# Dots of fetched rows queued later, and a tail of three combinations in a one-layer diffusion backbone with expert retrieval

## The chip, the cores and the metric

The kernel runs on one core of a Trainium2 chip. Its engines are TensorE (PE, with its weight loads as PEld), VectorE (DVE), ScalarE (ACT), GpSimd (POOL) and SyncE (SP, which here issues DMAs only). The metric is the device time of one execution in microseconds.

## The reference

One layer over 512 latent tokens of width 1024 with a prefix of 256 context tokens: a token mixer (two groups of linear-attention heads), then retrieval over 128 x 128 experts with one neuron each. The change touches the second half:

```python
def peer(h, w_query, sub_keys, expert_u, expert_v):
    def block(t):                                    # 128 tokens
        q = (t @ w_query).reshape(PEER_BLOCK, PEER_HEADS, 2, PEER_DQ // 2)
        s1 = jnp.einsum('thd,nd->thn', q[:, :, 0], k1)
        s2 = jnp.einsum('thd,nd->thn', q[:, :, 1], k2)
        v1, i1 = lax.top_k(s1, PEER_TOPK)
        v2, i2 = lax.top_k(s2, PEER_TOPK)
        ...
        top_s, pos = lax.top_k(cand_s, PEER_TOPK)    # 16 of 256 pairs
        idx = jnp.take_along_axis(cand_i, pos, axis=-1)
        g = jax.nn.softmax(top_s, axis=-1)
        act = jax.nn.gelu(jnp.einsum('thkd,td->thk', expert_u[idx], t))
        return jnp.einsum('thk,thkd->td', g * act, expert_v[idx])
```

Each token thus weighs 8 x 16 = 128 experts. A modulated residual and a layer norm follow.

## The kernel before

The 512 tokens are four blocks of 128. For blocks 0 to 2 (384 tokens, `TD`) the retrieval is done densely: every expert's hidden value for every token by matmul, times a gate that is zero for experts that weren't chosen. For block 3, and for the u side of the last 16 tokens of block 2 (`SH`, the shared tokens), the chosen rows of u and v are fetched one at a time.

**The choice.** DVE finds the top 16 of each list (`top16`, `pick_head`) and then the keys of the chosen pairs (`picks`: one-hot `oh`, times `spread`, summed to `key`), for block 2, then 3, then 0; block 1 follows within the gate matrix. In this part the order on DVE is written out by hand (a manual schedule), for DVE and later for DVE and POOL.

**The hidden blocks.** `hidden(n)` (64 of them, n = 0 to 63, two groups of 128 experts each) loads a megabyte `ur`, splits it into a high part `uh` (ACT) and a low part `ul` (DVE) in `load_split`, and runs 48 matmuls of 128 x 368 into `pH`, three for each product (`mm3`, lines 139 to 141: the high parts, and each low part with the other high one). ACT applies the gelu; 28 of the results (`SPILL`) go to DRAM (`Hd`) and come back later.

**The gate matrix.** `gate_block` makes for each of the three blocks 16 groups of 8 tokens; a group takes a one-hot product on DVE (lines 1093, 1098, 1104), four scaled copies on ACT (line 1100), and 24 matmuls into `pG` (line 1110). The results go through `stage` to DRAM (`Gd`), and come back for eight expert groups at a time as `Gn` (1536 KB).

**The fetched rows.** `fetched` is a generator of 272 steps, each of one 4 KB row for each of 128 tokens (512 KB): 16 for the shared tokens (`sdots`), then 16 of u and 16 of v in turn, 8 times. POOL issues the fetches into a ring of six buffers (`erow`), the first five at once and another as each dot is issued. A dot on DVE (lines 1221, 1227) reduces a row of u; line 1239 adds a weighted row of v into `yg`. After the 16 shared dots ACT takes their gelu and spreads them with eight small DMAs from its own queue (line 1225). How many rows are asked for at each place is set by `ROWS`: per group of the gate matrix, per half of a combination while hidden blocks remain, and per half of one after that. Ahead of the gate matrix there are rows in the choice: four between the steps of `picks(w, 3)` and one at each of the six steps of `picks(w, 0)`.

**The main loop.** Combination i (m = seq[i]) loads and splits a megabyte of v (`rows`: `vr`, `vh`, `vl`), multiplies the stored hidden values by the gates and splits them (`gated`: `gel`, `ah`, `al`), and adds 36 matmuls of 128 x 512 into the six accumulators `y` (`combine`). The first stage (i = 0 to 31) runs hidden block 32 + i on PE ahead of combination i; after the last one the ring of u (`uring`) is closed, and a second ring for v (`vring`) takes its place. From then on the loads of v alternate between the pools w and vring, two raw buffers and one pair of split tiles each. In this second stage eight loads of `w_g2` (1/8 of the last modulation each) also go through vring.

**The tail.** The last `TAIL` combinations are prepared together, and then run by block, so that block 0's sums end first; `finish` (residual, modulation, layer norm, lines 1251 to 1253 and 134 to 135, all on DVE) follows for block 3 (the fetched one), then 0, 1 and 2. Its modulation rows need `to_rows` (a transpose on PE, a copy on ACT at line 270) and two small DMAs on POOL. In the tail the order on ACT is that of the program. Elsewhere a scheduler sets the order by priorities of the program order.

Of the kernel before, what the change touches and what calls it, by code (L numbers as in the profile page):

```python
# [931 lines left out]
class Peer:  # L932
# [14 lines left out]
    LOOK = 5  # L947
    ROWS = (1.0, 2.75, 0.75)
    GB, OB = 8, 2
    GN = 8  # L950
    TAIL = 2

# [172 lines left out]

    def load_split(self, pool, src, tag, bufs):

        nc = self.nc
        raw = pool.tile([128, 2, 8, 128], F32, name=tag + "r", bufs=2)
        nc.sync.dma_start(raw, src)  # L1130
        parts = []
        for e in range(2):
            hi, lo = (pool.tile([128, 8, 128], F32R, name=tag + i, bufs=bufs) for i in "hl")
            nc.scalar.activation(hi, raw[:, e], AF.Copy)  # L1134
            self.mark = nc.vector.tensor_tensor(lo, raw[:, e], hi, op=OP.subtract).ins  # L1135
            parts.append((hi, lo))
        return parts
# [24 lines left out]

    def gated(self, n, pool, vpool, bufs, mark=None):

        nc = self.nc
        NG, NU = self.TD // self.GT, self.TU // self.GT
        if 2 * n % self.GN == 0:
            self.Gn = pool.tile([128, NG, self.GN, self.GT], F32, name="Gn", bufs=2)
            nc.sync.dma_start(self.Gn, self.Gd[:, :, 2 * n:2 * n + self.GN, :].rearrange("g m n t -> m g n t"))
        g = self.gel.pop(n)  # L1170
        g4 = g.rearrange("p n (g t) -> p n g t", t=self.GT)
        m = 2 * n % self.GN
        gates = self.Gn[:, :, m:m + 2, :].rearrange("p g n t -> p n g t")
        nc.scalar.activation(g4[:, :, NU:], gates[:, :, NU:], AF.Copy)
        with self.tc.issue_after(mark) if mark else ExitStack():
            nc.vector.tensor_tensor(g4[:, :, :NU], g4[:, :, :NU], gates[:, :, :NU], op=OP.mult)
        ah = vpool.tile([128, 2, self.TD], F32R, name="ah", bufs=bufs)
        al = vpool.tile([128, 2, self.TD], F32R, name="al", bufs=bufs)
        nc.scalar.activation(ah, g, AF.Copy)  # L1179
        nc.vector.tensor_tensor(al, g, ah, op=OP.subtract)  # L1180
        return ah, al

    def rows(self, n, pool):

        return self.load_split(pool, self.a["vd"][n], "v", 2)

# [8 lines left out]
    def fetched(self, w, ring, y):  # L1195
# [21 lines left out]
        for r, (src, j) in enumerate(order):  # L1217
# [8 lines left out]
            elif src == "u":  # L1226
                nc.vector.scalar_tensor_tensor(e, e, 1.0, h2, op0=OP.mult, op1=OP.mult, accum_out=dots[:, j:j + 1])  # L1227
                if j == 15:

                    g = self.g[96:128, 2].rearrange("p h k -> p (h k)")  # L1230
                    nc.vector.tensor_tensor(g, g, act[96:128], op=OP.mult)
                if j % 16 == 15:
                    sl = slice(j - 15, j + 1)
                    nc.scalar.activation(act[:, sl], dots[:, sl], AF.Gelu_apprx_tanh)
                    nc.vector.tensor_tensor(act[:, sl], act[:, sl], self.g[:, 3].rearrange("p h k -> p (h k)")[:, sl], op=OP.mult)
# [23 lines left out]
    def run(self, es, out):  # L1259
# [6 lines left out]
        kept, out_to = self.AHEAD, self.AHEAD + self.SPILL  # L1266
        seq = [*range(kept), *range(out_to, 64), *range(kept, out_to)]
        self.gel, self.last = {}, 2 * seq[-1]
        pers = es.enter_context(tc.tile_pool(name="pers", bufs=1, reuse_waits="tile"))
# [4 lines left out]
        with ExitStack() as e0:  # L1274
# [5 lines left out]
            with ExitStack() as e1:  # L1280
# [58 lines left out]
                for i, _ in enumerate(self.picks(w, 3)):  # L1339
                    if i % 2:  # L1340
                        more(0.5)
                    if i > 1:
                        next(fetched)
                index()
# [12 lines left out]
                with tc.tile_pool(name="bd", bufs=1, reuse_waits="tile") as bp:  # L1357
                    for i, _ in enumerate(self.picks(w, 0)):
                        if i % 2:
                            more(0.5)  # L1360
                        fetch(1)
                    more(0.5)
                    first, at, groups = asked, 0, ND * 128 // self.GB
                    for b in range(ND):
                        kg = self.picks_on_partitions(bp, ps, key2 if b == 2 else self.key, self.g[:, b])
                        following = self.picks(w, 1) if b == 0 else iter(())
# [8 lines left out]
            with ExitStack() as e1:  # L1375
# [5 lines left out]
                g2 = iter(())  # L1381
                vp, pools = None, [w]
                for i, m in enumerate(seq[:64 - self.TAIL]):
# [3 lines left out]
                    if nh < 64:  # L1387
                        self.hidden(nh, up, gl, hps)
                        nh += 1
                        if nh == 64:  # L1390
                            up_es.close()
                            deep = e0.enter_context(ExitStack())
                            vp = deep.enter_context(tc.tile_pool(name="vring", bufs=1, side="right", reuse_waits="tile"))
                            pools.append(vp)
                            g2 = n.mods_last(vp)
                    else:
                        next(g2, None)
                    fetch(rate)
                    v = self.rows(m, pools[i % len(pools)])
                    if nh == 64 and i + ahead < 64:  # L1400
                        self.back(seq[i + ahead], gl)
                    ops = self.gated(m, w, w, self.TAIL, mark), v
                    for e in range(2):
# [9 lines left out]
                for c, m in enumerate(tail):  # L1413
                    mark = self.mark
                    vs.append(self.rows(m, pools[(64 - self.TAIL + c) % 2]))
                    acts.append(self.gated(m, w, w, self.TAIL, mark))

# [48 lines left out]
```

## Time and profile before

| | |
|---|---|
| median of 3 runs | 1776.82 us (1775.97 to 1776.92) |
| the profiled execution | 1778.75 us |
| its span | 1776.8 us, 27590 instructions |
| mean granted TensorE clock | 0.973 |
| moved by DMA | 439.13 MB, mean 247 GB/s |
| PE idle, 600 to 700 us of the span | 19.3 us |
| longest single PE wait | 15.8 us, for `ul` |

The busy time of an engine counts its instructions from start to end; matmuls overlap, so a PE that is busy all the time is not at its peak. What limits a stage is read from the wait that ends last there. In a row of the timeline the columns are start, duration, engine, line, operation, output and inputs, shapes, count, and in brackets the idle time of the engine just before and what ended it. "SPq" and "ACTq" are DMAs issued by these engines.

### The profile page before, as it was taken

Reading aid. Unit: us, or ns where it says so; the run is one execution under the profiler, and the core shown is the slowest. Engines: PE = TensorE matmul, PEld = TensorE weight load, DVE = VectorE, ACT = ScalarE, POOL = GpSimd, SP = SyncE. Lnnn points to the kernel's source line nnn. Section 1 sums busy time; section 2 is a strip of 40 time slices with the busy share of each in tenths; the row PEclk is TensorE's granted clock in tenths of the full one; section 3 lists DMA queues with packets and bytes.
Section 4 is the critical chain, followed back from the end, with each engine's and each line's share of the span. In section 5 each row is a group of like instructions: output and inputs, shape, how many; then the busy total and the mean of one; then the engine's idle time right before and its main releaser. Section 6 shows DMA issues by size and latency. Waiting matters only on the chain. (4 is left out here: it accounts for less than half of the span.)

```text
span 1776.8 us, 27590 instructions
## 1 busy us (share of the span) xinstructions
PE 1669.0 (94%) x10440; PEld 1460.4 (82%) x10440; DVE 1450.7 (82%) x2824; ACT 831.2 (47%) x1413; POOL 483.1 (27%) x327
## 2 busy tenths in 40 slices
PE   6999999989999978999998999999999998999994
PEld 3888877876788978889898889999999997778883
DVE  6689888787799979999897788787787776677756
ACT  4667677664322354667574333243333333233331
POOL 0000000000043023126432555545455452223000
PEclk8999999989999998899999999999999999999997
DMA  8345345143331367799889999989989989999832
GB/s 320 121 140 175 123 136 179 48 191 117 125 108 52 116 208 276 275 321 328 309 328 372 337 374 359 320 325 347 352 304 340 345 296 331 329 309 339 292 126 95
DMA packets 155687, 439.13 MB, mean 247 GB/s; under 512 B 13105, under 2 KB 69777, under 8 KB 135074
## 3 DMA queue, kind: packets, MB, share of 16 engines
q1 hardware_dynamic: 114322, 289.94, 47.0%
q0 software_dynamic: 40400, 145.34, 22.5%
q10 hardware_dynamic: 832, 2.11, 0.3%
q8 instruction: 81, 1.33, 0.3%
q14 instruction: 52, 0.43, 0.1%
HBM read 388.93 MB, written 48.39 MB: 246 GB/s over the span
## 5 line engine op out<-in xcount | busy, mean ns | idle before, releaser
L141 PE MATMUL pH<-hh,ul 128*128 128x368 f32 x1024 | 342.7, 336 | 22.2 <-DVE ul L1135 22.1
L139 PE MATMUL pH<-hh,uh 128*128 128x368 f32 x1024 | 344.1, 336 | 5.7 <-ACT gel L1153 4.7
L140 PE MATMUL pH<-hl,uh 128*128 128x368 f32 x1024 | 341.3, 333 | 0.0
L139 PE MATMUL y<-vh,ah 128*128 128x512 f32 x768 | 300.2, 391 | 9.3 <-ACT vh L1134 5.7
L141 PE MATMUL y<-vh,al 128*128 128x512 f32 x768 | 298.9, 390 | 2.0 <-DVE al L1180 2.0
L140 PE MATMUL y<-vl,ah 128*128 128x512 f32 x768 | 299.9, 391 | 0.9 <-DVE vl L1135 0.8
L1212 POOL DMA_INDIRECT erow<-in_v_dram,ix x128 | 218.4, 1706 | 239.0 <-DVE yg L1239 133.6
L1212 POOL DMA_INDIRECT erow<-in_u_dram,ix x128 | 197.3, 1541 | 311.3 <-DVE erow L1227 178.6
L1135 DVE TENSOR_TENSOR vl<-vr,vh 128x1024 fp32r<-128x1024 f32 x128 | 156.0, 1222 | 108.9 <-ACT vh L1134 108.7
L1134 ACT ACTIVATE uh<-ur 128x1024 fp32r<-128x1024 f32 x128 | 135.3, 1059 | 206.8 <-PE pH L140 179.0
L1134 ACT ACTIVATE vh<-vr 128x1024 fp32r<-128x1024 f32 x128 | 134.3, 1054 | 186.2 <-PE y L141 115.5
L141 PEld LDWEIGHTS pH<-hh,ul 128*128 128x128 f32 x1024 | 195.4, 191 | 24.7 <-DVE ul L1135 24.6
L139 PEld LDWEIGHTS pH<-hh,uh 128*128 128x128 f32 x1024 | 195.6, 191 | 7.8 <-ACT gel L1153 5.3
L140 PEld LDWEIGHTS pH<-hl,uh 128*128 128x128 f32 x1024 | 195.7, 191 | 1.2
L139 PEld LDWEIGHTS y<-vh,ah 128*128 128x128 f32 x768 | 144.4, 188 | 39.9 <-ACT vh L1134 6.0
L141 PEld LDWEIGHTS y<-vh,al 128*128 128x128 f32 x768 | 144.6, 188 | 33.2 <-DVE al L1180 2.9
L140 PEld LDWEIGHTS y<-vl,ah 128*128 128x128 f32 x768 | 144.5, 188 | 30.6 <-DVE vl L1135 2.0
L1239 DVE SCALAR_TENSOR_TENSOR yg<-erow,q,yg 128x1024 f32<-128x1024 f32 x127 | 162.4, 1278 | 0.3
L1135 DVE TENSOR_TENSOR ul<-ur,uh 128x1024 fp32r<-128x1024 f32 x128 | 154.4, 1217 | 9.9 <-ACT uh L1134 9.9
L1227 DVE SCALAR_TENSOR_TENSOR erow<-erow,h 128x1024 f32<-128x1024 f32 x128 | 151.9, 1217 | 0.1
L1180 DVE TENSOR_TENSOR al<-gel,ah 128x768 fp32r<-128x768 f32 x64 | 61.0, 954 | 72.3 <-ACT ah L1179 72.1
L139 PE MATMUL pc<-hTh,wh 128*128 128x512 f32 (+1 forms) x304 | 110.2, 362 | 0.3 <-ACT G L379 0.3
(397 smaller groups left out, 3062.6 us busy)
## 6 DMA issues: line engine op xcount, KB each, us to landing
ur<-in_uT_dram SPq DMA_DIRECT2D x64, 1024.0 KB
vr<-in_vd_dram SPq DMA_DIRECT2D x64, 1024.0 KB
Gd<-stage SPq DMA_DIRECT2D x24, 1024.0 KB
Gn<-Gd SPq DMA_DIRECT2D x16, 1536.0 KB
wraw<-in_w_cf_dram SPq DMA_DIRECT2D x24, 512.0 KB
wada<-in_w_ada_dram SPq DMA_DIRECT2D x48, 256.0 KB
Hd<-gels SPq DMA_DIRECT2D x28, 368.0 KB
gel<-Hd SPq DMA_DIRECT2D x28, 368.0 KB
```

Source lines behind the costliest of these rows:

```text
L139: mm(out, lh, rh, start=start, stop=False)
L140: mm(out, lh, rl, start=False, stop=False)
L141: mm(out, ll, rh, start=False, stop=stop)
L1134: nc.scalar.activation(hi, raw[:, e], AF.Copy)
L1135: self.mark = nc.vector.tensor_tensor(lo, raw[:, e], hi, op=OP.subtract).ins
L1180: nc.vector.tensor_tensor(al, g, ah, op=OP.subtract)
L1212: nc.gpsimd.indirect_dma_start(out=e, out_offset=None, in_=a["v" if src == "v" else "u"], in_offset=bass.IndirectOffsetOnAxis(ap=ix[:, j:j ...
L1227: nc.vector.scalar_tensor_tensor(e, e, 1.0, h2, op0=OP.mult, op1=OP.mult, accum_out=dots[:, j:j + 1])
L1239: nc.vector.scalar_tensor_tensor(y, e, act[:, j:j + 1], y, op0=OP.mult, op1=OP.add)
```

## The change

Four things:

- The four rows in `picks(w, 3)` and the six in `picks(w, 0)` are no longer asked for there. The first call of the generator, which issues five fetches, stays where it was. `ROWS` becomes 0.85, 2.85 and 0.83.
- The product of the shared tokens' gates and hidden values (`g` for the last 16 tokens of block 2) is taken after the fifth row of u instead of the sixteenth, since rows come later; an assertion makes sure that it comes before block 2's part of the gate matrix.
- `TAIL` is 3 instead of 2. The third combination of the tail keeps its split v (`home[:2]`) and its split gated values (`home[2]`) in the memory of `hh` and `hl`, the split input that only the hidden blocks read. The buffers for `ah` and `al` stay at two.
- The loads of v alternate counted from i = 31 (`first`), so that combination 31 uses pool w and combination 32 is the first in vring.

```diff
-    ROWS = (1.0, 2.75, 0.75)
+    ROWS = (0.85, 2.85, 0.83)
-    TAIL = 2
+    TAIL = 3
...
-    def load_split(self, pool, src, tag, bufs):
+    def load_split(self, pool, src, tag, bufs, home=None):
...
-            hi, lo = (pool.tile([128, 8, 128], F32R, name=tag + i, bufs=bufs) for i in "hl")
+            hi, lo = home[e] if home else (pool.tile([128, 8, 128], F32R, name=tag + i, bufs=bufs) for i in "hl")
...
-        ah = vpool.tile([128, 2, self.TD], F32R, name="ah", bufs=bufs)
-        al = vpool.tile([128, 2, self.TD], F32R, name="al", bufs=bufs)
+        if home:
+            ah, al = (t.rearrange("p a b -> p (a b)")[:, 0:2 * self.TD].rearrange("p (e t) -> p e t", e=2) for t in home)
+        else:
+            ah, al = (vpool.tile([128, 2, self.TD], F32R, name=f"a{i}", bufs=bufs) for i in "hl")
...
-                if j == 15:
+                if j == 4:
                     g = self.g[96:128, 2].rearrange("p h k -> p (h k)")
                     nc.vector.tensor_tensor(g, g, act[96:128], op=OP.mult)
+                    self.shared = True
...
                 for i, _ in enumerate(self.picks(w, 3)):
                     if i % 2:
                         more(0.5)
-                    if i > 1:
-                        next(fetched)
...
                     for i, _ in enumerate(self.picks(w, 0)):
                         if i % 2:
                             more(0.5)
-                        fetch(1)
...
                     for b in range(ND):
+                        assert b < 2 or self.shared
...
                             pools.append(vp)
+                            first = i
...
-                    v = self.rows(m, pools[i % len(pools)])
+                    v = self.rows(m, pools[(i - first) % len(pools)])
...
-                    ops = self.gated(m, w, w, self.TAIL, mark), v
+                    ops = self.gated(m, w, w, self.TAIL - 1, mark), v
...
-                    vs.append(self.rows(m, pools[(64 - self.TAIL + c) % 2]))
-                    acts.append(self.gated(m, w, w, self.TAIL, mark))
+                    home = c == self.TAIL - 1 and [
+                        [t[:, 2 * j:2 * j + 2, :].rearrange("p a (b c) -> p (a b) c", c=128) for t in (self.hh, self.hl)]
+                        for j in range(3)]
+                    vs.append(self.rows(m, pools[(64 - self.TAIL + c - first) % 2], home and home[:2]))
+                    acts.append(self.gated(m, w, w, self.TAIL - 1, mark, home and home[2]))
```

The order of DVE's instructions in the middle of the choice (`erow,sdots` is a dot of a shared row, `oh` and `key` are the one-hot products and the result for block 3, `pr`, `pf` and `prf` small steps for the next blocks). Before, the stretch that holds the first three dots; the pair of splits (`ul`) follows eight rows later:

```order
L1030 TENSOR_SCALAR pr<-pos_5224 128x128 x3
L1221 SCALAR_TENSOR_TENSOR erow,sdots<-erow,yg 128x1024
L1054 TENSOR_TENSOR oh<-oh,spread 128x2048
L1056 TENSOR_TENSOR oh<-oh 128x8x128
L1056 TENSOR_TENSOR oh<-oh 128x8x64
L1056 TENSOR_TENSOR oh<-oh 128x8x32
L1057 TENSOR_TENSOR key<-oh 128x128
L1221 SCALAR_TENSOR_TENSOR erow,sdots<-erow,yg 128x1024
L1052 TENSOR_TENSOR oh<-prf,iota_5231 128x2048
L1221 SCALAR_TENSOR_TENSOR erow,sdots<-erow,yg 128x1024
L1054 TENSOR_TENSOR oh<-oh,spread 128x2048
L1043 SCALAR_TENSOR_TENSOR prf<-pf 128x128
```

And after, the stretch that ends with the same pair of splits:

```order
L1052 TENSOR_TENSOR oh<-prf,iota_5231 128x2048
L1030 TENSOR_SCALAR pr<-pos_5224 128x128
L1054 TENSOR_TENSOR oh<-oh,spread 128x2048
L1043 SCALAR_TENSOR_TENSOR prf<-pf 128x128
L1056 TENSOR_TENSOR oh<-oh 128x8x128
L1045 TENSOR_TENSOR prf<-pf 128x128
L1056 TENSOR_TENSOR oh<-oh 128x8x64
L1030 TENSOR_SCALAR pr<-pos_5224 128x128
L1056 TENSOR_TENSOR oh<-oh 128x8x32
L1040 CAST pf<-pr 128x512
L1057 TENSOR_TENSOR key<-oh 128x128
L1135 TENSOR_TENSOR ul<-ur,uh 128x1024 x2
```

Three dots stood ahead of this pair of splits and none does now. Ten of the dots ahead of the gate matrix have moved into it or behind it: the first dot stands at the end of the choice for block 0.

The loads on SP where the first stage ends (`silr` and `wg` belong to the last modulation). Before, the first load of vring stands ahead of `silr`:

```order
L1130 DMA vr<-in_vd_dram 128x2048
L1161 DMA gel<-Hd 128x2x368
L1130 DMA vr<-in_vd_dram 128x2048
L255 DMA silr<-sild 128x1024
L259 DMA wg_15062<-in_w_g_dram 128x1024
L1130 DMA vr<-in_vd_dram 128x2048
```

And after:

```order
L1130 DMA vr<-in_vd_dram 128x2048
L1161 DMA gel<-Hd 128x2x368 x2
L255 DMA silr<-sild 128x1024
L259 DMA wg_15032<-in_w_g_dram 128x1024
L1130 DMA vr<-in_vd_dram 128x2048
```

The first load of vring now stands behind the first load of w_g2 instead of ahead of both.

ACT in the tail, up to the copy of the last modulation row (line 270). Before:

```order
L1134 ACTIVATE vh<-vr 128x1024 x2
L1174 ACTIVATE gel<-Gn 128x2x16
L1179 ACTIVATE ah<-gel 128x768
L270 ACTIVATE q_4773<-prow 8x128
L1424 ACT_TABLE_LOAD
```

And after:

```order
L1134 ACTIVATE vh<-vr 128x1024 x2
L1174 ACTIVATE gel<-Gn 128x2x16
L1181 ACTIVATE ah<-gel 128x768
L1134 ACTIVATE hh<-vr 128x1024 x2
L1174 ACTIVATE gel<-Gn 128x2x16
L1181 ACTIVATE hh<-gel 128x768
L270 ACTIVATE q_4773<-prow 8x128
```

The third combination's four instructions, written into hh, stand ahead of that copy.

More of the change, by code (lines that the diff above doesn't have):

```diff
@@ L1161, in back, with gated @@
             self.nc.sync.dma_start(r[:, :, :self.TU], self.Hd[n - self.AHEAD])
-    def gated(self, n, pool, vpool, bufs, mark=None):
+    def gated(self, n, pool, vpool, bufs, mark=None, home=None):
         nc = self.nc
@@ L1181, in gated, with rows @@
         return ah, al
-    def rows(self, n, pool):
-        return self.load_split(pool, self.a["vd"][n], "v", 2)
+    def rows(self, n, pool, home=None):
+        return self.load_split(pool, self.a["vd"][n], "v", 2, home)
     def combine(self, n, e, b, ops, halves=(0, 1)):
@@ L1267, in run @@
         seq = [*range(kept), *range(out_to, 64), *range(kept, out_to)]
+        self.shared = False
         self.gel, self.last = {}, 2 * seq[-1]
@@ L1381, in run @@
                 g2 = iter(())
-                vp, pools = None, [w]
+                vp, pools, first = None, [w], 0
                 for i, m in enumerate(seq[:64 - self.TAIL]):
```

## The prediction

> **What bounds the kernel now.** I read the page first, then the busy time by windows, then PE's own timeline, because the page says that PE is the engine to follow.
>
> ```profile
> PE 1669.0 (94%) x10440; PEld 1460.4 (82%) x10440; DVE 1450.7 (82%) x2824; ACT 831.2 (47%) x1413; POOL 483.1 (27%) x327
> 600.00:700.00 100.00, 80.74 (x462) 79.21 (x462) 86.05 (x248) 45.44 (x51) 27.97 (x27) 0.91 0.64 219
> 1200.00:1300.00 100.00, 100.00 (x520) 90.97 (x519) 80.57 (x92) 36.46 (x50) 53.31 (x35) 1.00 0.93 343
> 1400.00:1500.00 100.00, 94.30 (x472) 83.95 (x471) 71.40 (x80) 33.65 (x47) 39.09 (x26) 0.97 0.91 326
> 1700.00:1777.00 77.00, 54.30 (x239) 44.17 (x237) 46.44 (x64) 18.16 (x27) 1.17 (x2) 0.88 0.30 107
> ```
>
> The columns are span, then busy time of PE, PEld, DVE, ACT and POOL, the granted clock, the DMA share and GB/s. PE has the same matmuls before and after, so a gain can only come from its idle time, from matmuls that run at a lower clock, or from the end, where DVE works alone. The steady stretch (1200 to 1300) has no PE idle at all. Three places have: the choice (19.3 us of idle in 600 to 700), the change from the first stage of the main loop to the second (5.7 in 1400 to 1500), and the end (22.7 in the last 77).
>
> **The choice.** PE's rows there, then DVE's in the same stretch:
>
> ```profile
> 655.35 0.33 PE L140 MATMUL pH<-hl,uh 128*128 128x368 f32 x1
> 671.45 0.68 PE L141 MATMUL pH<-hh,ul 128*128 128x368 f32 x1 [15.78 <-DVE ul L1135]
> 671.92 0.51 PE L139 MATMUL pH<-hh,uh 128*128 128x368 f32 x1
> 676.20 0.33 PE L141 MATMUL pH<-hh,ul 128*128 128x368 f32 x1
> ...
> 649.01 0.49 DVE L1030 TENSOR_SCALAR pr<-pos 128x128 uint32<-128x128 uint32 x3
> 659.27 1.23 DVE L1221 SCALAR_TENSOR_TENSOR erow<-erow,yg 128x1024 f32<-128x1024 f32 x1 [9.78 <-DMA erow<-in_u_dram,ixs]
> 660.42 1.29 DVE L1054 TENSOR_TENSOR oh<-oh,spread 128x2048 bf16<-128x2048 bf16 x1
> 663.26 0.29 DVE L1057 TENSOR_TENSOR key<-oh 128x128 f32<-128x128 bf16 x1
> 664.61 1.22 DVE L1052 TENSOR_TENSOR oh<-prf,iota 128x2048 bf16<-128x2048 bf16 x1
> 666.89 1.22 DVE L1054 TENSOR_TENSOR oh<-oh,spread 128x2048 bf16<-128x2048 bf16 x1
> 670.18 2.35 DVE L1135 TENSOR_TENSOR ul<-ur,uh 128x1024 fp32r<-128x1024 f32 x2
> ```
>
> DVE runs in order. At 649.5 it reaches the first dot of a fetched row, and the row lands only at 659.27. Behind that dot stand the rest of the third list's choice and the split ul that PE wants; PE stands for 15.78 us. After the change no dot stands there, as the order shows. What is left between 649.50 and the split is 3.05 us (660.42 to 663.47), 1.14 (664.61 to 665.75) and 3.29 (666.89 to 670.18): 7.5 in all. The split then starts at 657.0 and, at about 1.15 net each, is done at 658.1; PE waits from 655.67 to 658.1, 2.4 instead of 15.8. **Saved: 13.4.**
>
> The 15 matmuls from 671.45 to 676.20 take 4.75 us, and at the 0.17 of later ones they would take 2.6: the stall cost 2.15 more at a lower clock. Whether a stall of 2.4 still costs that, two rows bracket:
>
> ```profile
> 966.57 0.67 PE L139 MATMUL pH<-hh,uh 128*128 128x368 f32 x1 [2.33 <-ACT gel L1153]
> 973.62 0.50 PE L139 MATMUL y<-vh,ah 128*128 128x512 f32 x1 [2.19 <-ACT ah L1179]
> ```
>
> The first is slow (0.67 for the 0.33 of others), the second near normal. I take half, **1.1**, and keep 0 and 2.15 as ends. The Trainium skill (TensorE: Matmul & The Clock Gate, Part 1: The HAM clock gate) says that the array falls to half rate only after about 3.4 us of idle; by that the whole 2.15 would come back and the sum would be 1.05 lower, but the row at 966.57 is slow after 2.33, so the trace is not with it here.
>
> What is late next: the hidden blocks behind this one need two splits per 8 us of PE, and DVE has about 5 us of choice between them, so nothing in the choice stalls PE again. The gate matrix then starts some 14 us earlier on both DVE and PE. Counted in the order of DVE's instructions, its 48 groups have 37 dots between them instead of 44 (7 fewer of about 1.2), so DVE is no worse off. On POOL the queue keeps its order: the first five fetches go out where they did, the others as dots free their buffers, so rows wait in buffers for the dots and not the other way round. The reduction of the shared dots moves to the border of the first and second block; its eight DMAs on ACT's queue cost this much now:
>
> ```profile
> 730.83 1.32 ACT L1100 ACTIVATE ohg<-oh,g2f 128x128 bf16<-128x128 bf16 x4 [4.68 <-DMA q<-sdots]
> ```
>
> It stalls ACT in both kernels; for the whole gate matrix I take 0, with ends of -6 (7 dots fewer, 8.4 us of DVE, most of it under PE) and +6 (the 4.68, on PE, with the slow matmuls behind).
>
> **From the first stage to the second.** The transition on PE, SP and ACT:
>
> ```profile
> 1477.80 1.22 PE L139 MATMUL y<-vh,ah 128*128 128x512 f32 x2 [5.66 <-ACT vh L1134]
> 1481.76 0.40 PE L141 MATMUL y<-vh,al 128*128 128x512 f32 x1
> ...
> 1467.68 0.58 SPq L1130 DMA_DIRECT2D vr<-in_vd_dram  x1
> 1472.17 0.33 SPq L259 DMA_DIRECT2D wg<-in_w_g_dram  x1
> 1472.55 0.43 SPq L1130 DMA_DIRECT2D vr<-in_vd_dram  x1
> ...
> 1476.69 2.00 ACT L1134 ACTIVATE vh<-vr 128x1024 fp32r<-128x1024 f32 x2 [4.03 <-DMA vr<-in_vd_dram]
> ```
>
> Combination 31 is the first in the new pool, whose load goes out at 1467.68 and lands 9.0 us later, when PE has been ready since 1472.1. With first = 31 it is combination 32 that opens the pool, and PE has 8.2 us of combination 31 in between. Against that, its load now stands on SP behind the first w_g2 load, so it goes out like the one at 1472.55. Landing 9 us later, with the split of 1.1, gives 1482.6, where PE comes at 1480.3. So the 5.66 and the 1.9 of slow matmuls (nine in 3.96 us instead of 2.0) shrink to at most 2.3 and perhaps the slow ones. I take **5.0** off; the ends are 0 and 7.5.
>
> **The end.** PE, ACT and DVE:
>
> ```profile
> 1752.78 0.39 PE L139 MATMUL y<-vh,ah 128*128 128x512 f32 x1
> 1753.91 0.39 PE L141 MATMUL y<-vh,al 128*128 128x512 f32 x1
> ...
> 1738.81 0.85 ACT L1179 ACTIVATE ah<-gel 128x768 fp32r<-128x768 f32 x1
> 1739.56 0.25 ACT L270 ACTIVATE q<-prow 8x128 f32<-8x128 f32 x1
> ...
> 1739.84 0.95 DVE L1180 TENSOR_TENSOR al<-gel,ah 128x768 fp32r<-128x768 f32 x1
> 1747.58 1.29 DVE L1251 TENSOR_TENSOR vr<-yg,Gn 128x512 f32<-128x512 f32 x2 [6.79 <-DMA Gn<-m2d]
> 1772.11 1.41 DVE L135 SCALAR_TENSOR_TENSOR vr<-vr,q,Gn 128x512 f32<-128x512 f32 x2
> ```
>
> Five matmuls start within 1.13 us, 0.227 each; 36 make a combination of 8.2 and the 72 of the tail 16.3, so the tail starts at T = 1738.0. The copy of the last modulation row leaves ACT at T + 1.6, its row lands 8.0 later, and DVE then needs 25.9 for four blocks (1747.58 to 1773.52): T + 35.5. Afterwards the tail has 108 matmuls, and T lies 8.2 earlier against PE's end. ACT's program order puts the third combination's work ahead of that copy: two vh of about 1.0 to T + 3.6, the second split on DVE to 4.8, the product with the gates 0.9, then ah 0.85, so the copy comes at T + 6.5 and DVE ends at T + 6.5 + 8.0 + 25.9 = T + 40.4. PE itself waits some 4 us for that ah, which DVE's queue of finishes covers. Net 35.5 + 8.2 - 40.4 = **3.3** saved; the ends are 0 (every late ah counted on the end) and 8.2 (the copy no later than now).
>
> **What is added: rows late in the kernel.** Of 272 rows, the choice asks for 10 now and the gate matrix for 48 x 1.0, the first stage for 32 x 2 x 2.75: 234. Then it is 0, 48 x 0.85 and 32 x 2 x 2.85: 223. So 49 rows remain for the second stage instead of 38, at 1.66 a combination instead of 1.5. The first stage has 0.2 more a combination of 16 us, where PE has no idle time and DVE is busy for four fifths (the row at 1200 above): I take 0 there.
>
> ```profile
> vr<-in_vd_dram SPq DMA_DIRECT2D x64, 1024.0 KB
> Gn<-Gd SPq DMA_DIRECT2D x16, 1536.0 KB
> gel<-Hd SPq DMA_DIRECT2D x28, 368.0 KB
> 1652.15 0.23 ACT L1174 ACTIVATE gel<-Gn 128x32 f32<-128x32 f32 x1 [7.33 <-DMA Gn<-Gd]
> 1660.00:1680.00 20.00, 20.00 (x90) 16.57 (x89) 16.78 (x16) 7.35 (x10) 0.00 (x0) 1.00 0.97 316
> 1680.00:1700.00 20.00, 20.00 (x89) 16.54 (x89) 12.21 (x12) 7.74 (x9) 0.00 (x0) 1.00 0.45 153
> 1700.00:1710.00 10.00, 10.00 (x46) 8.28 (x45) 4.70 (x5) 3.77 (x4) 0.00 (x0) 1.00 0.77 268
> 1710.00:1720.00 10.00, 10.00 (x46) 8.29 (x45) 5.46 (x5) 3.00 (x4) 0.00 (x0) 1.00 0.20 83
> ```
>
> A combination needs 1024 + 368 + 384 KB and rows of 512 KB: 319 GB/s now, 330 then, with the queues at a share of 0.97 while they fetch. Eleven rows are 5.8 MB, 18 us at 320 GB/s; the room between 1680 and 1720 is 20 x 0.55 + 10 x 0.23 + 10 x 0.80 = 21. They fit, but not evenly: at 1652.15 the gates had kept ACT for 7.33 us, and ah came only 3.3 before PE wanted it. I take **+4** for gates that come too late, with 0 and 18 as ends. The Trainium skill (DMA: Bandwidth & Descriptors, Specifications) gives about 358 GB/s from HBM for a core; by that 330 would fit and the 4 would be 0, while the row at 0.97 with 316 says that these patterns fill the queues earlier.
>
> Three edits cost nothing at run time: the flag for the shared dots, the product of gates and shared dots after the fifth dot instead of the sixteenth (one small instruction on DVE, moved, ahead of the third block either way), and the place of the last combination in hh and hl, which nothing reads after the last hidden block at 1472; it gets the same two vh, ah and the same subtractions.
>
> The sum is -13.4 - 1.1 - 5.0 - 3.3 + 4 = **-18.8**. It is made against the profiled execution, 1778.75 us around a span of 1776.8; that is 1.9 above the median of the runs shown, so the forecast is 1776.82 - 18.8 = **1758.0**.
>
> **Rivals.** *DMA takes it back, and more* (slower). If the seven or so loads of gates in the second stage land 7 us later, PE stands 3.7 and runs slowly for 1.9 each time: 39 us, and 1776.8 - 22.8 + 39 = 1793. It decides from some 5 us of delay per load. For it speaks the share of 0.97; against it, that four combinations add only 0.33 MB, one us. Chance 0.07. *The room is just missed:* the 18 us come back whole, 1772 to 1778, no change that a measurement can tell; with it count a first dot that still holds DVE in the choice (the order speaks against it): 0.09. *ACT's eight DMAs stop PE at the border of the blocks:* +6, 1764 to 1770: 0.14. *More than I allow:* the idle of the gate matrix goes too (6), the transition wholly (2.5), and the rows hide (4): 1745: 0.15. *The forecast*, 1752 to 1764: 0.55.
>
> Faster by over 0.2% (3.6 us, about what a measurement of this kernel can tell) is 0.55 + 0.15 + 0.14 and a little of the second rival, 0.85; same 0.08; slower 0.07. The range leaves out the slower case and the outer half of the best: 1744 to 1772.
>
> **What would show it.** In the choice: no DVE row waiting for a fetched row, PE's wait before the split near 2.4, and the first gate group some 14 us earlier. At the transition a PE wait under 3. At the end DVE's first finish some 13 us after the tail starts on PE, with no gap behind it. In the second stage ACT's waits for Gn grow and PE's show at most two more. A PE wait of over 10 us left in the choice, or PE waits before each group of four combinations, would make this wrong.

## The result, and the profile after

The changed kernel took 1758.1 us in the median of four runs (1756.1 to 1761.0), beside 1776.6 for the kernel before (1776.0 to 1776.9): a ratio of 0.9898, with a 95% interval of 0.988 to 0.9915, so 18.5 us less. Run again later it gave 1760.0 beside 1778.1, 0.9909 (0.9882 to 0.9936). The forecast was 1758.0. That the total came out to 0.1 us is luck: of its terms one failed by 5 us, and others made up for it.

The profiled execution took 1756.08 us around a span of 1754.0. The line of busy times, and the windows (columns as before):

```profile
PE 1666.8 (95%) x10440; PEld 1456.8 (83%) x10440; DVE 1449.4 (83%) x2824; ACT 830.5 (47%) x1413; POOL 500.1 (29%) x327
600.00:700.00 100.00, 94.51 (x596) 91.81 (x594) 95.08 (x276) 55.37 (x74) 15.23 (x17) 0.98 0.57 199
1400.00:1500.00 100.00, 92.75 (x440) 80.27 (x439) 71.58 (x88) 31.48 (x42) 41.35 (x25) 0.97 0.91 315
1700.00:1754.00 54.00, 36.09 (x158) 28.97 (x157) 37.34 (x55) 11.40 (x21) 1.16 (x2) 0.86 0.23 81
```

In the window of the choice PE went from 80.7 to 94.5 us busy, and its clock from 0.91 to 0.98. In the window with the change of stages it did not gain: 92.8 busy, 94.3 before. The end is shorter.

To see where the time went, program points must be lined up, not times of the clock. I use ACT's rows at L1153, one per half of a hidden block, 128 in all. Of before, and then of after, halves 16, 20 and 76:

```profile
650.59 0.46 ACT L1153 ACTIVATE gels<-pH 128x368 f32<-128x368 f32 x1
686.37 0.46 ACT L1153 ACTIVATE gels<-pH 128x368 f32<-128x368 f32 x1
1065.84 0.46 ACT L1153 ACTIVATE gel<-pH 128x368 f32<-128x368 f32 x1
```

```profile
653.83 0.46 ACT L1153 ACTIVATE gels<-pH 128x368 f32<-128x368 f32 x1
674.00 0.46 ACT L1153 ACTIVATE gels<-pH 128x368 f32<-128x368 f32 x1
1043.77 0.46 ACT L1153 ACTIVATE gel<-pH 128x368 f32<-128x368 f32 x1
```

From half 16 to half 20 before took 35.8 us and after 20.2: the choice's gain lies there. The table gives the time between such rows for every profiled run below: up to half 16, 16 to 24 (the choice), 24 to 48 (gate matrix, first block and its border to the second), 48 to 56 (the next border), 56 to 76, 76 to the copy of the last modulation row (L270: 1739.56 before, 1718.25 after), and from there to the end of DVE's last row of `finish` ("end").

| run | to 16 | choice | 24–48 | 48–56 | 56–76 | 76 to copy | copy to end | end |
|---|---|---|---|---|---|---|---|---|
| before | 650.6 | 52.6 | 156.9 | 54.4 | 151.4 | 673.7 | 34.0 | 1773.5 |
| after | 653.8 | 36.4 | 154.7 | 48.7 | 150.1 | 674.5 | 32.4 | 1750.7 |
| again (after) | 650.5 | 35.7 | 156.4 | 49.1 | 151.5 | 673.8 | 32.4 | 1749.3 |
| choice_only | 649.6 | 34.8 | 149.6 | 49.6 | 152.3 | 678.1 | 34.4 | 1748.3 |
| first_four | 650.3 | 39.0 | 156.4 | 49.6 | 152.0 | 672.6 | 34.0 | 1753.9 |
| tail_only | 648.2 | 51.9 | 157.5 | 48.9 | 153.7 | 670.8 | 32.5 | 1763.6 |
| first_only | 648.6 | 52.7 | 157.3 | 48.9 | 155.2 | 671.4 | 32.8 | 1767.0 |
| old_rates | 652.0 | 34.8 | 148.3 | 49.8 | 152.2 | 667.8 | 32.6 | 1737.4 |
| sdots_pool | 650.0 | 34.8 | 147.9 | 53.3 | 150.4 | 674.7 | 33.0 | 1744.2 |
| more_rows | 653.7 | 35.9 | 150.8 | 50.3 | 150.6 | 666.3 | 32.8 | 1740.5 |
| third_rate | 651.3 | 35.0 | 154.4 | 48.3 | 151.2 | 668.8 | 32.7 | 1741.6 |
| more_late | 653.5 | 37.5 | 148.0 | 49.9 | 152.2 | 664.4 | 32.8 | 1738.4 |
| old_pool | 652.9 | 36.5 | 149.2 | 49.3 | 159.8 | 675.4 | 32.5 | 1755.6 |
| all_three | 650.6 | 34.8 | 149.5 | 51.5 | 151.1 | 663.1 | 32.8 | 1733.4 |

The first column shows how far one profile may be trusted: hardly anything is changed in that stretch, it spreads over 5.6 us, and the changed kernel run twice has 653.8 and 650.5. The column 48–56 holds a trap: before has 54.4 and most others 48 to 50, also tail_only and first_only, whose instructions stand there in the same order as before's. In before PE waits 3.50 at 871.86 for the next block's first one-hots, with 5.7 us of matmuls at half clock behind it; in tail_only and first_only that wait is 0.40 and 0.44. So some 5.5 of the 22.7 us by which the two profiles differ isn't shown to come from the change; the medians differ by 18.5. Whether before loses this in most of its executions or only in the profiled one stays open, and with it some 5 us of each comparison with before below.

**The choice.** PE's rows, and the split that PE had waited for:

```profile
659.09 0.43 PE L139 MATMUL pH<-hh,uh 128*128 128x368 f32 x1 [2.47 <-ACT gels L1153]
660.01 0.50 PE L141 MATMUL pH<-hh,ul 128*128 128x368 f32 x1 [0.32 <-DVE ul L1135]
...
658.74 2.35 DVE L1135 TENSOR_TENSOR ul<-ur,uh 128x1024 fp32r<-128x1024 f32 x2
```

The wait of 15.78 for the split is 0.32 now, and a wait of 2.47 for ACT stands ahead of it, where before had 1.02. The granted clock (the column behind the busy times) behind the wait, in before and then in after:

```profile
671.45:676.17 4.72, 4.72 (x15) 4.72 (x16) 4.72 (x8) 0.00 (x0) 1.92 (x2) 0.50 0.60 191
660.23:663.64 3.41, 3.41 (x12) 3.41 (x12) 3.41 (x5) 0.00 (x0) 2.80 (x3) 0.50 0.87 266
```

**The gate matrix.** The border of its first two blocks, on ACT and PE:

```profile
771.57 1.06 ACT L1134 ACTIVATE uh<-ur 128x1024 fp32r<-128x1024 f32 x1 [6.87 <-DMA q<-sdots]
772.89 0.43 ACT L1070 ACTIVATE kT<-pkT 128x128 bf16<-128x128 f32 x2
...
776.07 0.29 PE L1110 MATMUL pG<-ohg,oh 128*128 128x128 bf16 x2 [5.01 <-DVE ohg L1098]
```

ACT stands 6.87 us behind the shared dots' eight DMAs; the block's keys kT come only behind them, and PE waits 5.01 for the first one-hots.

**The change of stages** on SP, ACT and PE, and two later waits:

```profile
1437.28 0.38 SPq L1169 DMA_DIRECT2D Gn<-Gd  x1
1450.10 0.43 SPq L1130 DMA_DIRECT2D vr<-in_vd_dram  x1
...
1451.07 0.46 ACT L1153 ACTIVATE gel<-pH 128x368 f32<-128x368 f32 x1
1463.19 2.95 ACT L1134 ACTIVATE vh<-vr 128x1024 fp32r<-128x1024 f32 x3 [7.93 <-DMA vr<-in_vd_dram]
...
1464.30 2.92 PE L139 MATMUL y<-vh,ah 128*128 128x512 f32 x6 [6.05 <-ACT vh L1134]
1510.17 0.50 PE L139 MATMUL y<-vh,ah 128*128 128x512 f32 x1 [1.02 <-ACT ah L1181]
1513.03 0.51 PE L141 MATMUL y<-vh,al 128*128 128x512 f32 x1 [2.12 <-DVE al L1182]
```

The load for combination 32 has the extra cover that the prediction gave it, and PE waits 6.05, no less than the 5.66 before: the load takes 13.1 us from issue to use (1450.10 to 1463.19), where 9.0 were allowed.

**The end**, on PE, ACT and DVE:

```profile
1718.60 0.40 PE L139 MATMUL y<-hh 128*128 128x512 f32 x1
1735.70 0.39 PE L141 MATMUL y<-hh,hl 128*128 128x512 f32 x1
...
1718.25 0.25 ACT L270 ACTIVATE q<-prow 8x128 f32<-8x128 f32 x1
...
1724.73 1.29 DVE L1254 TENSOR_TENSOR vr<-yg,Gn 128x512 f32<-128x512 f32 x2 [5.39 <-DMA Gn<-m2d]
1749.27 1.41 DVE L135 SCALAR_TENSOR_TENSOR vr<-vr,q,Gn 128x512 f32<-128x512 f32 x2
```

Counted back from 1735.93, 108 matmuls of 0.2275 put the tail's start at T = 1711.4. The copy is at T + 6.9, DVE's first finish at T + 13.4, its end at T + 39.3, with no gap between.

### The profile page after: what moved, and what is told of

The parts are those of the page before. It is cut to its first block, busy times and chain, and to the rows that moved or that the text cites. A ratio compares the mean times of both kernels' runs of the same rounds, so it can differ in the third digit from the quotient of the medians.

```text
span 1754.0 us, 27581 instructions
## 1 busy us (share of the span) xinstructions
PE 1666.8 (95%) x10440; PEld 1456.8 (83%) x10440; DVE 1449.4 (83%) x2824; ACT 830.5 (47%) x1413; POOL 500.1 (29%) x327
## 3 DMA queue, kind: packets, MB, share of 16 engines
q0 software_dynamic: 40400, 145.34, 22.7%
## 5 line engine op out<-in xcount | busy, mean ns | idle before, releaser
L139 PE MATMUL pH<-hh,uh 128*128 128x368 f32 x1024 | 340.4, 332 | 3.2 <-ACT gels L1153 2.5
L1214 POOL DMA_INDIRECT erow<-in_v_dram,ix x128 | 231.2, 1806 | 255.8 <-DVE yg L1242 168.0
L1214 POOL DMA_INDIRECT erow<-in_u_dram,ix x128 | 202.6, 1583 | 254.6 <-DVE erow L1229 141.9
L1229 DVE SCALAR_TENSOR_TENSOR erow<-erow,h 128x1024 f32<-128x1024 f32 x128 | 151.4, 1219 | 1.8 <-DMA erow<-in_u_dram,ix 1.8
L140 PE MATMUL pc<-hTl,wh 128*128 128x512 f32 (+1 forms) x304 | 108.2, 356 | 0.0
```

The costliest lines, as they stand in the source:

```text
L139: mm(out, lh, rh, start=start, stop=False)
L140: mm(out, lh, rl, start=False, stop=False)
L1214: nc.gpsimd.indirect_dma_start(out=e, out_offset=None, in_=a["v" if src == "v" else "u"], in_offset=bass.IndirectOffsetOnAxis(ap=ix[:, j:j ...
```

## Experiments

Each ran three rounds beside the kernel before, whose medians in the three series were 1778.6, 1778.1 and 1773.9 us (single runs from 1771 to 1784).

**One part alone on the kernel before: the dots out of the choice.**

```diff
-                if j == 15:
+                if j == 4:
...
-                    if i > 1:
-                        next(fetched)
...
-                        fetch(1)
```

> The kernel before, with the ten dots taken out of the choice and the product with the shared dots moved to the fifth dot; rates, pools and tail as before. Theory (the first dot holds DVE's queue until its row lands, and that alone is the choice's stall): PE's wait of 15.8 us becomes about 2.5, some 2 us of slow matmuls go with it, so -15 to -16 by the choice; by the profile of the changed kernel the gate matrix then gives a few us more or less, since the border of its first two blocks took 5.0 there. -13 to -20 in all. Rival (the dots' own 10 x 1.2 us of DVE cost the time, and come back in the gate matrix): -3 to 0. Rival (the gain of the changed kernel comes from the rates, the pools and the tail): within 4 of before.

1754.6 us, ratio 0.9868 (0.984 to 0.9896). That is more than was expected: the choice's stretch is 17.8 shorter, and 24–48, where a gain was left open, 7.3; the stretch with the change of stages is 4.4 *longer*. This one part gives as much as the whole change; that it gives more isn't shown, since the intervals of the two overlap.

**Only the first four of the ten dots.**

```diff
-                    if i > 1:
-                        next(fetched)
```

> The kernel before, with only the four dots inside the choice of the third list taken out; the six of the next list stay. Theory (waiting in line for one late row): the first row lands some 10 us after its fetch goes out, at about 659, and the next list's first dot stands behind the third list's last steps, at about 658, so nearly the whole stall goes: -11 to -16. Rival (ten dots of 1.2 us each, in the way of the split): four tenths of it, -5 to -6.

1761.7 us, 0.9922 (0.9894 to 0.995), from 1759.3 to 1768.6; the choice's stretch is 13.6 shorter. DVE's rows where the first dot stands now:

```profile
655.25 2.35 DVE L1135 TENSOR_TENSOR ul<-ur,uh 128x1024 fp32r<-128x1024 f32 x2
...
657.73 1.21 DVE L1221 SCALAR_TENSOR_TENSOR erow<-erow,yg 128x1024 f32<-128x1024 f32 x1
```

The split runs at once, and the dot, now 2.5 us behind the split's start, finds its row there. Four dots of ten gave 13.6 of 17.8: it was the wait in line for one late row, not the dots' own work. The rival is out.

**Only the tail**, with `TAIL = 3`, the last combination in hh and hl, and two buffers of ah and al:

```diff
-    TAIL = 2
+    TAIL = 3
```

> The kernel before, with six combinations by block at the end instead of four, two of them kept in the place of h. The tail of the changed kernel ended 39.3 us after PE began it, with 8.2 us more of PE in it than before's 35.5. Theory (DVE's finishes start after the copy of the last modulation row, which comes about 5 us later, and PE's added 8.2 lie under them): -4 to -5. Rival (the tail's gain hangs on the earlier rows): 0.

1771.8 us, 0.9953 (0.9932 to 0.9973). The last two stretches lost 2.9 and 1.5: 4.4, as the theory has it. But the last one lies between 32.8 and 34.4 among kernels with the old tail, and the one before it is 1.1 shorter than before's in first_four, which changes nothing there. What is beyond doubt is the place of the copy: counted back from PE's last matmul, it stands 1.8 us behind the tail's start in all four profiles with the old tail and 6.9 behind it in all ten with the new one. That is 5.1 later against 8.2 more of PE in the tail, so 3.1 us. The median is 6.8 below before; the rest lies where nothing was changed.

**Only the pools' alternation.**

```diff
-                    v = self.rows(m, pools[i % len(pools)])
+                    v = self.rows(m, pools[(i - first) % len(pools)])
```

> The kernel before, with the first combination in the new pool one later. What the prediction held: the load has 8 us more of cover, PE's wait of 5.66 falls under 2.3, -5. What the changed kernel's profile suggests (its load lay 13.1 us from issue to landing behind two loads of hidden rows, the conditioning row and the first weights, and PE waited 6.05): within 1.5 of before, with PE's wait at 4 to 7.

1769.7 us, 0.9953 (0.9936 to 0.9971). Its load of gates on SP, the last half of a hidden block on ACT, and PE's wait; then PE's wait in choice_only:

```profile
1449.46 0.38 SPq L1169 DMA_DIRECT2D Gn<-Gd  x1
1469.10 0.48 ACT L1153 ACTIVATE gel<-pH 128x368 f32<-128x368 f32 x1 [1.41 <-PE pH L141]
1480.25 2.93 PE L139 MATMUL y<-vh,ah 128*128 128x512 f32 x6 [3.02 <-ACT vh L1134]
```

```profile
1449.97 1.22 PE L139 MATMUL y<-vh,ah 128*128 128x512 f32 x2 [7.81 <-ACT vh L1134]
```

Neither forecast held: the wait is 3.02, and the median is 8.9 below before, of which the wait explains 2.6 (the stretch 48–56, where nothing was changed, is 5.5 shorter). So the new alternation does gain 2.6 here, and the dots' move alone costs 2.2 (7.81 for 5.66). What differs is Gn's load. Here it goes out 19.6 us ahead of the last half; in the changed kernel 13.8 (1437.28 to 1451.07), and in choice_only 13.6. DVE's rows ahead of the product that frees Gn's buffer, in the changed kernel and then in first_only:

```profile
1435.19 1.22 DVE L1229 SCALAR_TENSOR_TENSOR erow<-erow,h 128x1024 f32<-128x1024 f32 x1
1436.34 0.92 DVE L1176 TENSOR_TENSOR gel<-gel,Gn 128x736 f32<-128x736 f32 x1
```

```profile
1447.32 1.28 DVE L1239 SCALAR_TENSOR_TENSOR yg<-erow,q,yg 128x1024 f32<-128x1024 f32 x1
1448.52 0.92 DVE L1176 TENSOR_TENSOR gel<-gel,Gn 128x736 f32<-128x736 f32 x1
```

With ten rows fewer behind it, DVE is in a batch of dots (L1229) where before it was in a batch of sums (L1239). Behind the last split of v, six dots stand ahead of the product; of the sums one. (Each sum needs the one before it, and a dot needs none; that the scheduler therefore puts more dots there is likely, but not shown.) Gn's load of 1.5 MB then falls in with the new pool's first loads. That is tested below, with as many rows as before.

**The changed kernel again**, unchanged.

> The changed kernel itself, beside the other three on one chip: 1756 to 1761, as in its first runs. Its sections tell which of its differences come again: the 3.7 us that the last 28 combinations before the tail lost (PE's wait of 6.05 at the change of stages) and the 5.0 at the border of the first two blocks should; the 2.6 late before the choice and the 5.5 gained at the border of the last two blocks should not be tied to the change.

1760.0 us. The border's wait came again with 5.22, the change of stages with 4.98; the late start did not. The short 48–56 came again too (49.1), as in most kernels.

**The rates of before.**

```diff
-    ROWS = (0.85, 2.85, 0.83)
+    ROWS = (1.0, 2.75, 0.75)
```

> The changed kernel with the rates of before (1.0, 2.75, 0.75; 224 rows by the end of the first stage for 223). Theory (the rates moved the shared dots' eight DMAs to the border of the first two blocks, where kT waits behind them): that wait of 5.0 with its 2 us of slow matmuls goes, the change of stages stays bad (6 to 8): 1750 to 1753. Rival (the border costs the same wherever the DMAs stand): as the changed kernel, 1756 to 1760.

1745.9 us, 0.9836 (0.9805 to 0.9867): 14 below the changed kernel beside it. Gates 24–48 lost 8.1 and the wait at the border went, as the theory has it; but the stretch with the second stage lost 6.0 too, which it had not forecast (the third rate below shows where that comes from).

**The shared dots' DMAs on POOL's queue.**

```diff
-                        nc.scalar.dma_start(act[128 - SH:128, q * SH:(q + 1) * SH], ...)
+                        nc.gpsimd.dma_start(act[128 - SH:128, q * SH:(q + 1) * SH], ...)
```

> The changed kernel with the shared dots' eight DMAs on POOL's queue instead of ACT's. Theory (PE's 5.0 at the border are ACT's queue held by them): it shrinks to the 1.1 to 1.4 of the next border, -4 to -6 against the changed kernel. Rival (the border waits for the kT and the first one-hots of the block anyway): within 2 of it. The rows that POOL fetches behind them come up to 8 us later, which the dots feel if five rows ahead aren't enough.

1749.8 us, 0.9849 (0.9818 to 0.9879). That is 10 below the changed kernel beside it, more than the forecast, and the rival is out. Gates 24–48 are 147.9 for 156.4: at the first border PE's wait is 0.34. The next border, however, took

```profile
845.48 0.40 PE L1110 MATMUL pG<-ohg,oh 128*128 128x128 bf16 x2 [6.54 <-DVE ohg L1098]
```

where the changed kernel had 1.06; two later runs with POOL's queue (2.22 and 1.99) did not show it. So the profile ties about 4 us net to the queue, and where the rest of the medians' 10 lies stays open.

**As many rows by the end of the first stage as before.**

```diff
-    ROWS = (0.85, 2.85, 0.83)
+    ROWS = (1.0, 2.9, 0.75)
```

> The changed kernel with the rates 1.0, 2.9 and 0.75: the first stage ends at row 233 as before did (234), not 223, so that sums and not dots stand on DVE when the stages change, and 39 rows are left for the second stage. Theory (dots run ahead of the product with the gates on DVE; Gn's buffer comes free 6 us late and its load of 1.5 MB falls in with the first loads of the new pool): Gn's load goes out some 6 us earlier, PE's wait of 6.05 becomes about 3.0 as with the pools alone, the second stage has one or two late gates fewer; with the border's gain of the old rate 1747 to 1751. Rival (the wait hangs on the loads of the new pool alone): PE's wait stays at 6 to 8, 1751 to 1755.

1746.7 us, 0.9832 (0.9797 to 0.9867). Gn's load, the first use of the new pool's load, and PE's wait; the last half is at 1447.62:

```profile
1427.98 0.38 SPq L1169 DMA_DIRECT2D Gn<-Gd  x1
1458.70 2.96 ACT L1134 ACTIVATE vh<-vr 128x1024 fp32r<-128x1024 f32 x3 [5.93 <-DMA vr<-in_vd_dram]
...
1459.81 1.97 PE L139 MATMUL y<-vh,ah 128*128 128x512 f32 x6 [4.06 <-ACT vh L1134]
```

Gn goes out 19.6 ahead again, as the theory says, and the wait shrinks, to 4.06 and not to 3.0. PE's wait at the change of stages, over all runs but the two below in which that first load was moved ahead:

| | Gn out 19.6 ahead | Gn out 13.6 to 14.7 ahead |
|---|---|---|
| old alternation | 5.66, 5.88, 5.64 | 7.81 |
| new alternation | 3.02, 4.06 | 6.05, 4.98, 5.27, 5.87, 5.39, 5.39 |

The alternation gives about 2.3 in either column, Gn's delay takes about 2 in either row: together nothing. (One cell has a single run.)

**The third rate alone as before** (0.75 for 0.83).

> The changed kernel with the third rate alone as before (0.75 for 0.83: 1.5 rows a combination for 1.66 in the second stage). Theory (rows late: at the higher rate the fetches run into the gates' loads, PE waits for ah and al near combination 36 and runs slowly behind): the waits of 1 to 2.4 at 1510 and 1513 and the slow matmuls go, the stretch from the last hidden block to the copy of the last modulation row is 5 to 7 shorter, and the border of the first two blocks keeps its 5: 1752 to 1755. Rival (what the second stage lost came with the rates of the first stage, by the phase of the rows): as the changed kernel, 1757 to 1761.

1749.1 us, 0.9859 (0.9826 to 0.9892), 3 below what was expected; but the kernel before was 4 lower in this series too. PE's waits at the border and in the second stage:

```profile
771.58 0.39 PE L1110 MATMUL pG<-ohg,oh 128*128 128x128 bf16 x2 [4.51 <-DVE ohg L1098]
1513.80 0.50 PE L141 MATMUL y<-vh,al 128*128 128x512 f32 x1 [0.35 <-DVE al L1182]
```

The border keeps its wait; the pair of late gates near 1510 is down to 0.35, and the stretch is 5.0 shorter than in the run again (5.7 than in after). So 1.66 rows a combination instead of 1.5 cost that. (It is one profile each: old_pool below has the rate 0.75 too and 675.4 in this stretch, with other waits.)

**The first load ahead of the last modulation's**, on more_rows:

```diff
-                    else:
+                    elif i > first + 1:
                         next(g2, None)
```

> The run with rates 1.0, 2.9 and 0.75, and the last modulation's loads begun one combination later, so that the first load into the new pool stands ahead of the conditioning row and the first weights on SP. Theory (at the change of stages the transfers share one full path, and this load waits for 1 MB ahead of it): PE's wait of 4.06 shrinks to 0 to 1.5 and the slow matmuls behind it go, -3 to -5 against that run (1742 to 1744). Rival (it waits for the place in the pool or for loads before those): PE's wait stays at 3 to 4, within 1.5 of it.

1742.7 us, 0.9816 (0.9784 to 0.9849). SP's order, the load's first use on ACT, and PE's waits:

```profile
1446.68 0.59 SPq L1130 DMA_DIRECT2D vr<-in_vd_dram  x1
1447.39 0.37 SPq L255 DMA_DIRECT2D silr<-sild  x1
1447.80 0.42 SPq L259 DMA_DIRECT2D wg<-in_w_g_dram  x1
...
1455.59 2.95 ACT L1134 ACTIVATE vh<-vr 128x1024 fp32r<-128x1024 f32 x3 [2.87 <-DMA vr<-in_vd_dram]
...
1456.70 0.51 PE L139 MATMUL y<-vh,ah 128*128 128x512 f32 x1 [0.99 <-ACT vh L1134]
1457.96 0.50 PE L140 MATMUL y<-vl,ah 128*128 128x512 f32 x1 [0.76 <-DVE vl L1135]
```

PE's 4.06 became 0.99 and 0.76; the slow matmuls behind it stayed in this profile (granted clock 0.50 from 1458.48 to 1461.89) and are gone in all_three. The last half stands at 1447.57 and 1447.62 in the two runs, so the load goes out 1.1 us earlier than in more_rows (0.9 ahead of it for 0.2 behind it) and is used 3.1 earlier. The other 2 us were the megabyte ahead of it on its queue. The Trainium skill (DMA: Bandwidth & Descriptors, Queues, rings and completion order) says that on each engine the descriptors of one issuer's queue are consumed in order; this pair of runs agrees with it. This is the lowest median of all, below both kernels with intervals that don't meet. That it is lower than more_rows is shown by the wait alone: the 4.0 between the medians are 2.8 when each is measured against the kernel before beside it, and the two intervals overlap.

**Rates of before, and POOL's queue.**

> The changed kernel with the rates of before and the shared dots' DMAs on POOL's queue. Theory (at the old rate ACT's DMAs stand behind kT and under other waits, so they cost PE next to nothing there): within 3 of the run with the old rates alone, 1743 to 1748. Rival (they still cost there what the queue of POOL saved at the new rate, 7 to 8 in the first block and its border): 1738 to 1740.

1753.5 us, 0.986 (0.9813 to 0.9908), from 1743.0 to 1760.7, the profiled run being the slowest. Gates 24–48 took 149.2 for 148.3: POOL's queue gives nothing at this rate. What made the profiled run slow lies behind, a wait of 4.58 for a split at

```profile
930.11 0.67 PE L141 MATMUL pH<-hh,ul 128*128 128x368 f32 x1 [4.58 <-DVE ul L1135]
```

and late gates in the second stage. Whether POOL's queue brings these stays open.

**All three.**

> Rates 1.0, 2.9 and 0.75, the first load ahead of the last modulation's, and the shared dots' DMAs on POOL's queue: the best that the runs suggest. By the sums of the theories 1739 to 1744; if the queue of POOL gives nothing at these rates, as the run before.

1746.8 us, 0.9849 (0.9814 to 0.9884), from 1738.5 to 1750.6. The profile is that of the fastest run, with waits of 0.75 and 0.77 at the change of stages. In the median POOL's queue added nothing to more_late, and its runs spread further.

## Why the prediction was right, and where it was not

**The choice** (-13.4 of wait, -1.1 of slow matmuls): the mechanism was right, first_four shows it, and the size was some 2 too small. The stretch lost 16.2, 16.9 when run again. PE's waits in it, summed over its rows, went from 16.8 to 3.0 and 1.5, so -13.8 and -15.3. I had left 2.4 for the split; with no dot in line, and none of the steps held up behind it, the split was done as PE came to it (0.32), and what is left of PE's waits is for ACT. By the granted clock PE worked 4.7 us at half speed in this stretch before, 3.4 in after and none when run again, so the lower clock gave back 0.7 and 2.4: the 1.1 lies between. Some 1.7 of after's gain is left without a cause, and the run again gained 0.8 less than these terms.

**The gate matrix** (0, ends -6 and +6): the stretches 24–48 and 56–76 moved by -3.4 together, and by -0.4 in the run again. The zero was right, as a sum of two things. (What the prediction counts as 44 and 37 dots are rows of both kinds: DVE's rows show 29 dots and 15 sums within the gate matrix before, 29 and 7 after, so the fewer ones are all sums.) The wait for the shared dots' DMAs left the first block and came up at its border; the rival that named ACT's eight DMAs had the place right. It was taken as an addition of 6; in truth it was the old cost, moved. And it was not needed: with the old first rate the DMAs stand behind kT in ACT's order, and 24–48 is 8 shorter (148.0 to 150.8 in all six profiles with the ten dots moved and the rate 1.0; 154.4 to 156.4 in the three with 0.85 and ACT's queue). The prediction kept the three rates for a matter of how many rows are left, and did not ask what the first of them puts next to the border.

**The change of stages** (-5.0) is the step that failed: "Landing 9 us later, with the split of 1.1, gives 1482.6". The landing took 13.1, and the gain was nothing: 5.66 before, 6.05 and 4.98 after. The extra cover is real: the new alternation was worth 2.3 to 2.6 by itself (first_only, and the columns of the table). Two things took the rest: the megabyte that the change puts ahead of that load, which the prediction named and priced at nothing but the later issue (more_late: 2.3 us of PE's waits), and Gn's load 6 us late, because other rows stand on DVE at that moment (about 2 us by the rows of the table). I had counted how many rows are left, not which kind is in line where.

**Rows late** (+4, ends 0 and 18): right in sign and near in size. Behind the change of stages PE waits 3.4 us in before and none of its work is slow; in after it waits 4.6 and works 3.4 at half clock, so 2.9 is lost, and 3.4 when run again. ACT's waits for Gn grew as forecast, from 46 to 54. But it was not a price of the rows that are left: third_rate leaves the same 49 for the second stage, and PE waits 1.8 there. The price was that of the 0.08 in the rate.

**The tail** (-3.3): right, 3.1 by the place of the copy (T + 6.9 for T + 1.8 before, counted alike). The last row landed 6.5 behind the copy for 8.0, another 1.5 that isn't shown to be the tail's: it lies between 6.9 and 8.4 with the old tail, and between 6.4 and 7.1 with the new. PE did not wait 4 us for the third combination's ah: the matmuls of other blocks were put ahead, and the first that reads hh stands at 1718.60, just as ah is ready.

The stretches add up: -16.2 for the choice, -3.4 for the gate matrix, +3.9 from half 76 to the copy without the tail (where I had -5.0 + 4.0), -3.1 for the tail and -1.5 for the landing are -20.3, against the forecast's -18.8; the rest of the profiles' 22.8 is +3.2 at the start and -5.7 at the border 48–56, neither shown to come from the change.

## What to carry to other kernels

An engine that runs in order pays for a late operand with everything behind it: move the instruction that waits behind work that is ready, and count the wait, not the instruction. Moving work shifts the phase of all that follows; look at what it then stands next to (a border, a buffer that must come free, the first loads of a new pool), since gains of 2 to 8 us were lost or found there by a rate that only seemed to say how much is done where. Compare stretches between the same instructions, and first measure how far a stretch that no one touched moves by itself.

## Not expected of the hardware

The lower clock does not begin when PE does. In more_late PE comes back from a wait of 3.19 at full speed, and turns slow 1.4 us later:

```profile
941.64 0.43 PE L139 MATMUL pH<-hh,uh 128*128 128x368 f32 x1 [3.19 <-ACT gel L1153]
...
943.08 0.51 PE L141 MATMUL pH<-hh,ul 128*128 128x368 f32 x1
```

In the changed kernel the wait of 2.12 at 1513.03, 2.9 us behind one of 1.02, is followed by slow matmuls (0.63 for 0.39) from 1513.62 to 1517.0, although neither wait reached 2.2. The Trainium skill (TensorE: Matmul & The Clock Gate, Part 1: The HAM clock gate) has the clock follow a free-running window of about 3.4 us; the late onset agrees with a window, while these two rows are slow without any idle time of that length.

What a short wait costs beyond itself can't be read from its own length; where it falls says more. In each profile the granted clock changes on one grid of 3.41 us: every half-clock stretch from 600 us to the tail starts on it and lasts a whole number of steps. A wait of 2.29 in the choice lies within one step in more_late, and is split between two in all_three:

```profile
656.35:659.76 3.41, 0.81 (x4) 0.37 (x3) 3.41 (x10) 3.22 (x3) 2.79 (x3) 1.00 0.42 132
659.76:663.18 3.42, 3.42 (x11) 3.42 (x12) 3.42 (x5) 0.00 (x0) 2.81 (x3) 0.50 0.89 279
...
651.52:654.93 3.41, 2.04 (x13) 1.74 (x11) 3.41 (x9) 1.88 (x2) 1.12 (x2) 1.00 0.01 3
654.93:658.35 3.42, 2.18 (x11) 1.88 (x12) 3.42 (x7) 1.81 (x3) 2.81 (x3) 1.00 0.88 194
658.35:661.76 3.41, 3.41 (x23) 3.41 (x22) 3.41 (x5) 1.20 (x2) 2.80 (x3) 1.00 0.92 363
```

The first is idle for 2.6 of its step, and the next step runs at half clock; the second is idle for 1.4 and 1.2, and nothing follows. Over the fourteen profiles, from 600 us to the tail, all 54 full-clock steps with at least 1.9 us of idle PE were followed by a half-clock one, none of those with under 1.5, and 5 of the 25 between. The limit is an estimate from these rows, since the ends of matmuls are modelled. It also tells apart the two rows between which the prediction took the half: the wait of 2.33 put 2.1 us of idle time into one step, the wait of 2.19 only 1.7.
